# Query products of both layers in plain float32 from an unsplit copy of the normed input; in layer 1 the expert blocks computed ahead as well

## The chip, the cores and the metric
The kernel runs on one core of one Trainium2 chip. The metric is the device time of one execution in microseconds. A core has TensorE (PE; its weight loads are PEld), VectorE (DVE), ScalarE (ACT), GpSimd (POOL) and SyncE (SP), which issues most of the DMAs.

## What is computed
Two layers of a hybrid diffusion backbone on 256 latent and 256 context tokens of width 1024. A layer is a mixer sublayer (four groups of heads, an output projection, a residual and a layer norm) and then an expert layer with product keys, which is the part that the change touches:
```python
def block(hb):                       # 128 tokens, hb: normed and modulated input
    q = (hb @ wq).reshape(PEER_BLOCK, PEER_HEADS, 2, PEER_QDIM // 2)
    s = jnp.einsum('thpk,hpnk->thpn', q, sub_keys).astype(jnp.float32)
    v1, i1 = lax.top_k(s[:, :, 0], K)
    v2, i2 = lax.top_k(s[:, :, 1], K)
    cand = (v1[..., :, None] + v2[..., None, :]).reshape(PEER_BLOCK, PEER_HEADS, K * K)
    cv, ci = lax.top_k(cand, K)
    e = ...                          # expert number from i1, i2 at ci
    g = jax.nn.softmax(cv, -1).reshape(PEER_BLOCK, PEER_HEADS * K)
    act = jax.nn.gelu(jnp.einsum('td,ted->te', hb, u_tab[e]).astype(jnp.float32))
    w = (g * act).astype(hb.dtype)
    return jnp.einsum('te,ted->td', w, v_tab[e])
```
There are 8 heads, 128 keys per half, 16384 experts and 16 picks per head. Layer 0 works on all 512 tokens (four tiles of 128), layer 1 on the 256 latent ones (two tiles).

## The kernel before, in words
All arithmetic is float32. A large product is made of three instructions per 128 rows of the contraction: each operand is split into a rounded half `hi` and a remainder `lo` of type float32r, and `mm3` (L140 to L143) adds hi x hi, hi x lo and lo x hi. `split` (L136 to L138) makes the halves: a cast on ScalarE (L137) and a subtraction on VectorE or GpSimd (L138). Small products (scores, transposes, the modulation products at L260) take unsplit float32 operands.

The expert layer runs in these steps.
- `to_hT` (L781) transposes the normed tokens `x_n` on TensorE, applies scale and shift into `h` on VectorE and ScalarE in turn, and splits `h` into the two halves `hT[0]` and `hT[1]`. In layer 0 it also transposes tile 3 back for the gathered path (`h2n`).
- The routing loop `for q in range(17)` (L1137) alternates `wq(q)` (L1038: load 512 KB of weights into `w_raw`, split with the subtraction on GpSimd, 8 x `mm3` over all NT columns, 512 in layer 0 and 256 in layer 1, copy `qs`) and `top(q - 1)` (L1046: the score product `ss`, a copy to one of two `s_` buffers, and five VectorE instructions per tile for the 16 best). After each four, `pairs(j)` (L1071) combines the halves of two heads on VectorE. One step of the modulation products (`next(fill)`) is made per round in layer 0; `fill_to` (L1150) makes the rest after the loop.
- `u_stage(bl)` (L1006) computes block `bl` of 128 experts for all dense tokens (384 columns in layer 0, where tile 3 takes the gathered path, 256 in layer 1): load `u_raw`, split it, 8 x `mm3` into the bank `au`, gelu into `act`. Of the 128 blocks, 26 in layer 0 and 38 in layer 1 are computed ahead (UA + UB): UA (2, 12) right after the routing loop, UE (7, 6) before the first gates, one after a set of gates where `UM` says so, the others after all gates. GpSimd makes most of their subtractions.
- `slots` (L1172) transposes the picks (`tr`), `hots` (L1182) makes hot rows, and `gates(t, tb)` (L1198) multiplies them on VectorE (L1206, L1209; two buffers each), adds them on TensorE (bank `G`), copies to `stg` and stores to `Gd` in DRAM: 8 per tile.
- The main loop (L1345) computes block `st` ahead by UA + UB, multiplies block `bl` of `act` by its gates (loaded from `Gd` into `gt`), splits the result and the value rows (`v_raw`) and adds into `ov`. The last two blocks are added tile by tile at the end.

`u_raw` is a ring of 2 buffers in layer 0 and 3 in layer 1; `w_raw` of 3. The loads of `u_raw` are issued behind the last `wq` load (`late["D"]`), all on SyncE's queue. A scheduler orders each engine's instructions when the kernel is built, after a time line of its own, with the order of the program as priority; the engines then run their queues in that order.

Of the kernel before, what the change touches and what calls it, by code (L numbers as in the profile page):

```python
# [45 lines left out]
WHB = (4, 5)  # L46
WB = 3
FL = 6
FM = 11
LF = 200  # L50
NF = 2
HB = 3
# [31 lines left out]
def tile_hybrid_diffusion(ctx: ExitStack, tc: tile.TileContext, I: dict, out: bass.AP):  # L84
# [695 lines left out]

    def to_hT(tiles, xsrc, cc, hT, p, back=None, hb=2):  # L781

        for t in tiles:
            s = t // 2
            for q in range(2):
                b = bank("xT")
                for j in range(4):
                    k = 4 * q + j
                    T.transpose(b[:, j * 128:(j + 1) * 128], xsrc(t)[:, k * 128:(k + 1) * 128], ident)
                h = mk(p, [128, 4, 128], tag="h", bufs=hb)  # L790
                for j in range(4):
# [6 lines left out]
                sl = slice(t * 128, t * 128 + 128)  # L798
                split(h, hT[0][:, 4 * q:4 * q + 4, sl], hT[1][:, 4 * q:4 * q + 4, sl])
                if back and t in back:  # L800
# [42 lines left out]
    for l in range(2):  # L843
# [161 lines left out]

        def u_stage(bl, eng=None):  # L1006
            raw = mk(up, [128, 8, 128], tag="u_raw", bufs=URB[l])
            with tc.issue_after(late["D"].ins):
                nc.sync.dma_start(raw, I["uT"][l, bl])
            hi = mk(up, [128, 8, 128], F32R, tag="u_hi", bufs=2 + l)  # L1010
            lo = mk(up, [128, 8, 128], F32R, tag="u_lo", bufs=2 + l)
            split(raw, hi, lo, eng)
            b = bank("au")
            for k in range(8):
                mm3(b[:, :ND], hi[:, k, :], lo[:, k, :], hT[0][:, k, :ND], hT[1][:, k, :ND], k == 0, k == 7)
            p, n = rings[0] if bl % (UA[l] + UB[l]) < UA[l] else rings[1]
            a = mk(p, [128, ND], tag="act", bufs=n)
            S.activation(a, b[:, :ND], AF.Gelu_apprx_tanh)
            acts[bl] = a

        with ExitStack() as rt:
            rp = pool("rp", stack=rt)
            sl4 = mk(rp, [128, NTL, 4, 8, 16], name="sl4")
            dec = mk(rp, [128, 3, 16], F16, name="dec")
            nc.sync.dma_start(dec, I["dec"])
            with ExitStack() as wqs:
                wp = pool("wq", bufs=2, stack=wqs)
                rp2 = pool("rp2", bufs=1, stack=wqs)
                if l:
                    prep.clear()  # L1030
                    prep.update(raw=(wp, 2))
                to_hT(range(NTL), lambda t: x_n[:, t, :], lnc, hT, rp2, {3: h2n} if GT else None, HB)
                keys = mk(rp2, [128, 16, 128], tag="keys", bufs=1)
# [4 lines left out]
                def wq(q):  # L1038
                    hi, lo = load_w(wp, I["wq"][l, q], bufs=WB)
                    b = bank("pq")  # L1040
                    for k in range(8):
                        mm3(b[:, :NT], hi[:, k, :], lo[:, k, :], hT[0][:, k, :NT], hT[1][:, k, :NT], k == 0, k == 7)
                    sq[q] = mk(rp2, [128, NT], tag="qs", bufs=2)
                    S.copy(sq[q], b[:, :NT])
# [107 lines left out]
                for bl in range(UA[l]):  # L1152
                    u_stage(next(ahead), G)
            xp_s.close()
# [66 lines left out]
            for _ in range(UE[l]):  # L1221
                u_stage(next(ahead), V if UEV[l] else G)
            for i, t in enumerate(DT):
                for tb in range(8):
                    gates(t, tb, *cur)
                    if i + 1 < len(DT):
                        if tb == 2:
                            nxt = slots(DT[i + 1])
                        elif tb == 7:
                            nxt = hots(nxt)  # L1230
                    if tb % 8 in UM[l]:
                        for bl in ahead:
                            u_stage(bl, G)
                            break
                cur = nxt
            for bl in ahead:
                u_stage(bl)

# [290 lines left out]
```

## Time and profile before
| | us |
|---|---|
| three runs: lowest, median, highest | 2938.61, 2943.63, 2950.1 |
| the profiled execution | 2948.22 |
| its span, first to last instruction | 2946.4 |

Busy in the profiled execution: TensorE 2656.8 us (90% of the span), VectorE 2099.5 (71%), ScalarE 1164.1 (40%), GpSimd 778.3 (26%). Its mean granted TensorE clock is 0.957 of full speed. In time: layer 0's mixers to 400 us, its routing to 623, gates and blocks ahead to 805, main loop to 1750; layer 1's mixers to 2045, routing to 2187, gates and blocks ahead to 2323, main loop to the end.

A chain of waits names, from the end backwards, what released each step. Matmuls are pipelined: a busy time of TensorE holds the tail of its last instruction, and the pitch of a series is read from the starts.

### The profile page before, as it was taken

The numbers are of one execution on the slowest core, as the hardware profiler recorded it, in microseconds if no ns is written. First come the engines' busy times: TensorE is split into PE (matmuls) and PEld (weight loads), VectorE is DVE, ScalarE is ACT, GpSimd is POOL, SyncE is SP. The second block draws the span as 40 slices with busy tenths as digits, with TensorE's granted clock in tenths as the row PEclk, the third lists the DMA queues.
The fourth block names the chain that finished last, engine by engine and source line by source line (L and its number), as shares of the span: only waits on it lengthen the run. The fifth ranks groups of instructions, "written<-read, shape, count | busy, mean of one in ns | idle before, by whom it ended". The sixth has DMA issues, their size and how long they took to land.

```text
span 2946.4 us, 41926 instructions
## 1 busy us (share of the span) xinstructions
PE 2656.8 (90%) x15646; PEld 2286.7 (78%) x15646; DVE 2099.5 (71%) x4255; ACT 1164.1 (40%) x1810; POOL 778.3 (26%) x505
## 2 busy tenths in 40 slices
PE   6798879688899999999999998788778999999997
PEld 3674557478899988888888987656777999999986
DVE  4956448989687778777767646964999865555556
ACT  2333533235433333333333334334345544444443
POOL 2333013134224444444334103321564100000000
PEclk9899989889899999999999999998888999999999
DMA  7122434336899999988889645325336986666656
GB/s 255 57 90 94 150 122 137 112 117 245 286 334 311 326 321 321 319 307 302 305 308 308 200 129 179 119 82 183 115 116 231 319 272 202 217 209 210 200 181 197
DMA packets 241840, 625.08 MB, mean 212 GB/s; under 512 B 22424, under 2 KB 104794, under 8 KB 236004
## 3 DMA queue, kind: packets, MB, share of 16 engines
q1 hardware_dynamic: 201156, 475.05, 48.6%
q0 software_dynamic: 40480, 147.36, 14.1%
q8 instruction: 122, 2.00, 0.3%
q14 instruction: 82, 0.67, 0.1%
HBM read 573.04 MB, written 49.30 MB: 211 GB/s over the span
## 4 chain that ended last, share of the span: by engine, by line
PE 46%; DVE 20%; DMA 14%; issue 12%; POOL 5%; ACT 3%; SPq 0%; POOLq 0%; DVEq 0%; ACTq 0%
DMA grow<-in_vg_dram,eu 8%; PE ov L142 6%; PE ov L141 6%; PE ov L143 5%; POOL grow L1311 5%; PE au L141 4%; PE au L143 4%; PE au L142 4%; DVE yT L365 2%; PE pj L141 1%; PE pj L142 1%; PE pj L143 1%; DMA wa_raw<-in_w_ada_dram 1%; DVE accg L1324 1%; DVE e L1067 1%
## 5 line engine op out<-in xcount | busy, mean ns | idle before, releaser
L143 PE MATMUL au<-hT,u_lo 128*128 128x384 f32 (+1 forms) x2048 | 642.0, 314 | 12.6 <-POOL u_lo L138 10.0
L141 PE MATMUL au<-hT,u_hi 128*128 128x384 f32 (+1 forms) x2048 | 645.4, 315 | 6.4 <-ACT u_hi L137 3.4
L142 PE MATMUL au<-hT,u_hi 128*128 128x384 f32 (+1 forms) x2048 | 641.5, 313 | 0.0
L142 PE MATMUL ov<-v_lo,wh 128*128 128x512 f32 x1280 | 505.2, 395 | 28.2 <-DVE v_lo L138 27.8
L143 PE MATMUL ov<-v_hi,wl 128*128 128x512 f32 x1280 | 500.1, 391 | 0.0
L141 PE MATMUL ov<-v_hi,wh 128*128 128x512 f32 x1280 | 462.9, 393 | 5.9 <-ACT wh L137 5.6
L137 ACT CAST u_hi<-u_raw 128x1024 fp32r<-128x1024 f32 x256 | 268.7, 1050 | 496.1 <-PE au L142 319.8
L141 PEld LDWEIGHTS au<-hT,u_hi 128*128 128x128 f32 x2048 | 394.1, 192 | 15.3 <-ACT u_hi L137 4.2
L143 PEld LDWEIGHTS au<-hT,u_lo 128*128 128x128 f32 x2048 | 393.2, 192 | 15.6 <-POOL u_lo L138 10.9
L142 PEld LDWEIGHTS au<-hT,u_hi 128*128 128x128 f32 x2048 | 394.1, 192 | 7.7
L138 DVE TENSOR_TENSOR v_lo<-v_raw,v_hi 128x1024 fp32r<-128x1024 f32 x255 | 312.8, 1227 | 79.4 <-ACT v_hi L137 79.1
L138 DVE TENSOR_TENSOR u_lo<-u_raw,u_hi 128x1024 fp32r<-128x1024 f32 x198 | 242.0, 1222 | 148.1 <-ACT u_hi L137 148.1
L137 ACT CAST v_hi<-v_raw 128x1024 fp32r<-128x1024 f32 x256 | 268.3, 1048 | 143.2 <-DMA v_raw<-in_v_dram 109.5
L142 PEld LDWEIGHTS ov<-v_lo,wh 128*128 128x128 f32 x1280 | 241.8, 189 | 84.2 <-DVE v_lo L138 40.9
L137 ACT CAST wh<-act 128x384 fp32r<-128x384 f32 (+1 forms) x256 | 116.9, 459 | 431.1 <-PE ov L142 419.7
L141 PEld LDWEIGHTS ov<-v_hi,wh 128*128 128x128 f32 x1280 | 242.0, 190 | 51.4 <-ACT wh L137 5.9
L143 PEld LDWEIGHTS ov<-v_hi,wl 128*128 128x128 f32 x1280 | 241.5, 189 | 49.7
L138 POOL TENSOR_TENSOR w_lo<-w_raw,w_hi 128x1024 fp32r<-128x1024 f32 (+1 forms) x72 | 176.9, 2466 | 251.5 <-ACT w_hi L137 219.6
L138 POOL TENSOR_TENSOR u_lo<-u_raw,u_hi 128x1024 fp32r<-128x1024 f32 x58 | 171.4, 2961 | 257.3 <-ACT u_hi L137 250.8
L1311 POOL DMA_INDIRECT grow<-in_vg_dram,eu x128 | 179.0, 1398 | 221.5 <-DVE accg L1324 167.2
L1311 POOL DMA_INDIRECT grow<-in_ug_dram,eu x128 | 160.6, 1255 | 262.8 <-DVE grow L1315 232.2
L1324 DVE SCALAR_TENSOR_TENSOR accg<-grow,ag,accg 128x1024 f32<-128x1024 f32 x127 | 162.8, 1282 | 75.8 <-DMA grow<-in_vg_dram,eu 75.1
(832 smaller groups left out, 4324.9 us busy)
## 6 DMA issues: line engine op xcount, KB each, us to landing
u_raw<-in_uT_dram SPq DMA_DIRECT2D x256, 512.0 KB
v_raw<-in_v_dram SPq DMA_DIRECT2D x256, 512.0 KB
Gd<-stg SPq DMA_DIRECT2D x40, 1024.0 KB
gt<-Gd SPq DMA_DIRECT2D x80, 512.0 KB
wa_raw<-in_w_ada_dram SPq DMA_DIRECT2D x76, 512.0 KB
w_raw<-in_w_in_t_dram SPq DMA_DIRECT2D x44, 512.0 KB
w_raw<-in_wq_dram SPq DMA_DIRECT2D x32, 512.0 KB
w_raw<-in_w_ada_dram SPq DMA_DIRECT2D x20, 512.0 KB
```

Of the source, the lines that this page charges most:

```text
L137: S.copy(hi, src)
L138: late["V" if eng in (None, V) else "G"] = (eng or V).tensor_tensor(lo, src, hi.bitcast(F32), ALU.subtract)
L141: T.matmul(o, lh, rh, start=first, stop=False)
L142: T.matmul(o, lh, rl, start=False, stop=False)
L143: return T.matmul(o, ll, rh, start=False, stop=last)
L365: V.scalar_tensor_tensor(uc, upad[:, m, :, j:j + 256], wj, uc, op0=ALU.mult, op1=ALU.add)
L1067: V.tensor_tensor(x[:, :, :, 0:w], x[:, :, :, 0:w], x[:, :, :, w:2 * w], ALU.add)
L1311: nc.gpsimd.indirect_dma_start(out=r, out_offset=None, in_=I[tab], in_offset=bass.IndirectOffsetOnAxis(ap=eu[:, i:i + 1], axis=0))
L1324: V.scalar_tensor_tensor(accg, r, ag[:, i:i + 1], accg, op0=ALU.mult, op1=ALU.add)
```

## The change
With `PW` the routing of both layers keeps an unsplit copy of the normed input, `h32` (in layer 0 tiles 0 to 2; tile 3 in `h32g`), and `wq` multiplies the raw weights by it in plain float32, with `w_raw` as a ring of 4 and 5 buffers (`PRB`) and no halves of the weights. The halves `hT`, which the blocks need, are made from the copy after product 1, in four pieces, with the subtraction on VectorE; those of layer 0's tile 3, which only the query products read, are gone. With `PU` the 38 blocks ahead of layer 1 are plain too: no `u_hi`, no `u_lo`, `u_raw` read by TensorE. The blocks of layer 0 and those of both main loops stay split.
```diff
--- before.py
+++ after.py
@@ -45,6 +45,9 @@
 NE = 2
 WHB = (4, 5)
 WB = 3
+PW = (1, 1)
+PU = (0, 1)
+PRB = (4, 5)
 FL = 6
 FM = 11
 LF = 200
@@ -778,7 +781,7 @@
         run(ssd(), attention(), hyena(), conf_norm(), more)
         mp_s.close()
 
-    def to_hT(tiles, xsrc, cc, hT, p, back=None, hb=2):
+    def to_hT(tiles, xsrc, cc, hT, p, back=None, hb=2, h32=None):
 
         for t in tiles:
             s = t // 2
@@ -787,7 +790,7 @@
                 for j in range(4):
                     k = 4 * q + j
                     T.transpose(b[:, j * 128:(j + 1) * 128], xsrc(t)[:, k * 128:(k + 1) * 128], ident)
-                h = mk(p, [128, 4, 128], tag="h", bufs=hb)
+                h = h32(t)[:, 4 * q:4 * q + 4, :] if h32 else mk(p, [128, 4, 128], tag="h", bufs=hb)
                 for j in range(4):
                     k = 4 * q + j
                     sc, sh = cc[:, 0, k, s:s + 1], cc[:, 1, k, s:s + 1]
@@ -796,7 +799,8 @@
                     else:
                         V.tensor_scalar(h[:, j, :], b[:, j * 128:(j + 1) * 128], sc, sh, op0=ALU.mult, op1=ALU.add)
                 sl = slice(t * 128, t * 128 + 128)
-                split(h, hT[0][:, 4 * q:4 * q + 4, sl], hT[1][:, 4 * q:4 * q + 4, sl])
+                if not h32:
+                    split(h, hT[0][:, 4 * q:4 * q + 4, sl], hT[1][:, 4 * q:4 * q + 4, sl])
                 if back and t in back:
                     b = bank("hb")
                     for j in range(4):
@@ -1003,16 +1007,24 @@
         rings = [(up, UA[l])]
         gsl = {}
 
-        def u_stage(bl, eng=None):
+        def u_stage(bl, eng=None, plain=False):
             raw = mk(up, [128, 8, 128], tag="u_raw", bufs=URB[l])
             with tc.issue_after(late["D"].ins):
                 nc.sync.dma_start(raw, I["uT"][l, bl])
+            if plain:
+                b = bank("au")
+                for k in range(8):
+                    T.matmul(b[:, :ND], raw[:, k, :], h32[0][:, k, :ND], start=k == 0, stop=k == 7)
+                return act_of(bl, b)
             hi = mk(up, [128, 8, 128], F32R, tag="u_hi", bufs=2 + l)
             lo = mk(up, [128, 8, 128], F32R, tag="u_lo", bufs=2 + l)
             split(raw, hi, lo, eng)
             b = bank("au")
             for k in range(8):
                 mm3(b[:, :ND], hi[:, k, :], lo[:, k, :], hT[0][:, k, :ND], hT[1][:, k, :ND], k == 0, k == 7)
+            act_of(bl, b)
+
+        def act_of(bl, b):
             p, n = rings[0] if bl % (UA[l] + UB[l]) < UA[l] else rings[1]
             a = mk(p, [128, ND], tag="act", bufs=n)
             S.activation(a, b[:, :ND], AF.Gelu_apprx_tanh)
@@ -1022,6 +1034,9 @@
             rp = pool("rp", stack=rt)
             sl4 = mk(rp, [128, NTL, 4, 8, 16], name="sl4")
             dec = mk(rp, [128, 3, 16], F16, name="dec")
+            h32 = []
+            if PW[l]:
+                h32.append(mk(rp, [128, 8, ND], name="h32"))
             nc.sync.dma_start(dec, I["dec"])
             with ExitStack() as wqs:
                 wp = pool("wq", bufs=2, stack=wqs)
@@ -1029,17 +1044,35 @@
                 if l:
                     prep.clear()
                     prep.update(raw=(wp, 2))
-                to_hT(range(NTL), lambda t: x_n[:, t, :], lnc, hT, rp2, {3: h2n} if GT else None, HB)
+                if PW[l] and GT:
+                    h32.append(mk(rp2, [128, 8, 128], name="h32g"))
+
+                def cols32(t):
+                    return h32[1] if t in GT else h32[0][:, :, t * 128:(t + 1) * 128]
+                to_hT(range(NTL), lambda t: x_n[:, t, :], lnc, hT, rp2, {3: h2n} if GT else None, HB, cols32 if PW[l] else None)
                 keys = mk(rp2, [128, 16, 128], tag="keys", bufs=1)
                 nc.sync.dma_start(keys, I["keys"][l])
                 n8 = 2 * NTL
                 vs, ixs, sq = {}, {}, {}
 
                 def wq(q):
-                    hi, lo = load_w(wp, I["wq"][l, q], bufs=WB)
                     b = bank("pq")
-                    for k in range(8):
-                        mm3(b[:, :NT], hi[:, k, :], lo[:, k, :], hT[0][:, k, :NT], hT[1][:, k, :NT], k == 0, k == 7)
+                    if PW[l]:
+                        raw = mk(wp, [128, 8, 128], tag="w_raw", bufs=PRB[l])
+                        late["D"] = nc.sync.dma_start(raw, I["wq"][l, q])
+                        o = 0
+                        for h in h32:
+                            n = h.shape[-1]
+                            for k in range(8):
+                                T.matmul(b[:, o:o + n], raw[:, k, :], h[:, k, :], start=k == 0, stop=k == 7)
+                            o += n
+                        if q == 1:
+                            for i in range(0, 8, 2):
+                                split(h32[0][:, i:i + 2, :], hT[0][:, i:i + 2, :ND], hT[1][:, i:i + 2, :ND])
+                    else:
+                        hi, lo = load_w(wp, I["wq"][l, q], bufs=WB)
+                        for k in range(8):
+                            mm3(b[:, :NT], hi[:, k, :], lo[:, k, :], hT[0][:, k, :NT], hT[1][:, k, :NT], k == 0, k == 7)
                     sq[q] = mk(rp2, [128, NT], tag="qs", bufs=2)
                     S.copy(sq[q], b[:, :NT])
 
@@ -1150,7 +1183,7 @@
                 fill_to(1, (FL, 11)[l])
                 ahead = iter(range(min(UA[l] + UB[l], 128)))
                 for bl in range(UA[l]):
-                    u_stage(next(ahead), G)
+                    u_stage(next(ahead), G, PU[l])
             xp_s.close()
             if l == 0:
                 fwp_s.close()
@@ -1219,7 +1252,7 @@
 
             cur = hots(slots(DT[0]))
             for _ in range(UE[l]):
-                u_stage(next(ahead), V if UEV[l] else G)
+                u_stage(next(ahead), V if UEV[l] else G, PU[l])
             for i, t in enumerate(DT):
                 for tb in range(8):
                     gates(t, tb, *cur)
@@ -1230,11 +1263,11 @@
                             nxt = hots(nxt)
                     if tb % 8 in UM[l]:
                         for bl in ahead:
-                            u_stage(bl, G)
+                            u_stage(bl, G, PU[l])
                             break
                 cur = nxt
             for bl in ahead:
-                u_stage(bl)
+                u_stage(bl, None, PU[l])
 
 
         UBl = UA[l] + UB[l]
```

## Rows read from the trace of the kernel before
**Rows 1.** By stretch: busy us of PE, PEld, DVE, ACT, POOL; clock, DMA share, GB/s
```profile
437.00:520.00 83.00, 81.12 (x424) 59.34 (x424) 71.09 (x383) 27.23 (x38) 30.17 (x12) 1.00 0.43 138
520.00:607.00 87.00, 59.05 (x358) 39.33 (x357) 84.48 (x521) 19.46 (x25) 5.77 (x3) 0.77 0.38 127
2055.00:2186.00 131.00, 100.41 (x734) 97.64 (x734) 120.10 (x536) 55.15 (x88) 67.19 (x27) 0.88 0.36 116
2186.00:2214.00 28.00, 20.24 (x148) 20.14 (x149) 23.67 (x20) 10.80 (x17) 20.17 (x7) 0.80 0.45 139
2214.00:2306.00 92.00, 80.17 (x879) 77.69 (x879) 85.83 (x53) 51.67 (x94) 35.91 (x13) 0.93 0.70 241
2323.00:2900.00 577.00, 575.87 (x3535) 518.15 (x3535) 353.03 (x572) 278.90 (x416) 6.79 (x9) 1.00 0.69 222
```
**Rows 2.** Instructions of L1116, 2055 to 2310 us: duration in ns, min/median/max, first and last start
```profile
L1116 DVE TENSOR_TENSOR e<-e,dec x4: 674/1750/2914, 2092.1 to 2179.3; 128x1024 f16<-128x1024 f16 x4
```
**Rows 3.** Timeline, 2150 to 2160 us: start, length, engine, line, instruction, [idle before]
```profile
2150.80 7.58 POOL L138 TENSOR_TENSOR u_lo<-u_raw,u_hi 128x1024 fp32r<-128x1024 f32 x3 [3.38 <-ACT u_hi L137]
...
2153.23 2.91 DVE L1116 TENSOR_TENSOR e<-e,dec 128x1024 f16<-128x1024 f16 x1
```
**Rows 4.** Groups of GpSimd, 2045 to 2323 us: busy us, mean ns | idle before, releasers
```profile
L138 POOL TENSOR_TENSOR u_lo<-u_raw,u_hi 128x1024 fp32r<-128x1024 f32 x34 | 91.6, 2702 | 89.9 <-ACT u_hi L137 85.9 <-PE au L142 2.2 <-PE G L1216 1.8
```
**Rows 5.** Chain of waits, 395 to 660 us (layer 0): start, length in us, what
```profile
410.62 2.76 DVE hT L138
...
423.51 0.72 PE pq L141 x2
...
453.05 0.89 PE ss L1050 x8
...
460.31 0.89 PE ss L1050 x8
...
568.03 0.89 PE ss L1050 x8
...
569.55 3.64 DMA wa_raw<-in_w_ada_dram
...
623.17 0.45 PE tr L1175
```
**Rows 6.** Timeline of TensorE: plain float32 products of 512, 256 and 128 columns
```profile
223.06 1.98 PE L528 MATMUL uf<-yT,dft 128*128 128x512 f32 x4
...
276.25 1.89 PE L555 MATMUL yi<-dft,hT 128*128 128x256 f32 x8
...
434.92 1.05 PE L1050 MATMUL ss<-keys,qs 128*128 128x128 f32 x8
```
**Rows 7.** Timeline of TensorE, from 2141 us: split products of 256 columns
```profile
2140.81 0.28 PE L143 MATMUL au<-hT,u_lo 128*128 128x256 f32 x1
2140.93 0.28 PE L141 MATMUL au<-hT,u_hi 128*128 128x256 f32 x1
```
**Rows 8.** Chain of waits, 2035 to 2420 us (layer 1): start, length in us, what
```profile
2055.26 0.58 PE pq L142
...
2066.17 0.44 PE ss L1050 x4
2069.43 0.44 PE ss L1050 x4
...
2186.76 0.48 PE tr L1175
...
2214.50 0.59 PE G L1215 x4
...
2307.20 7.69 DMA Gd<-stg
...
2315.37 6.88 DMA v_raw<-in_v_dram
...
2323.38 1.19 PE ov L141 x4
```

## The prediction
> **What bounds the kernel now.** I read the busy time by stretch first, then the chain of waits through the two routing stages, then the timeline. Each layer ends in a long expert loop that TensorE fills: in layer 1 it is busy 575.87 of 577 us at a granted clock of 1.00 (2.4 GHz) [rows 1]. So whatever brings the start of that loop forward comes off the end, and whatever delays it is added. The change touches only what stands ahead of the two loops: query products with their top-16 search ("routing"), gates, and blocks computed ahead. There it is not TensorE that is full. From 2055 to 2306 us TensorE is busy 100 of 131, 20 of 28 and 80 of 92 us, at mean granted clocks of 0.88, 0.80 and 0.93, while VectorE is busy 120, 24 and 86 [rows 1]; the chain there runs almost wholly through VectorE. In layer 0 TensorE is full from 437 to 520 (81 of 83), then VectorE is (84 of 87) [rows 1].
>
> VectorE is partly held up. The same comparison (L1116, 1024 columns) takes 674 ns at its fastest and 2914 at its slowest, among four in layer 1 [rows 2], and the slow one begins at 2153.23, while GpSimd runs three `u_lo` subtractions from 2150.80 to 2158.38 [rows 3]. I took each VectorE instruction's duration less the tenth percentile of its own form. The excess is 45 us between 2055 and 2186, 41 us from there to 2310 and 31 us in layer 0 between 437 and 623. Nearly all of it lies on instructions with two tensors as input and on copies, casts and scalar forms; the `MAX8` searches lose next to nothing. GpSimd has 34 `u_lo` subtractions in layer 1's stretch [rows 4] and 16 of `w_lo`, one per query product: 86 / 50 = 1.7 us lost per subtraction, between 0 and 2.2 (2914 less 674) by the row. The Trainium skill (SBUF — State Buffer, Who interferes with whom) says that the two engines share one pair of ports, held for a whole instruction. By that rule, which the rows bear out, the excess goes with the subtractions.
>
> **The change, part by part.**
> (a) *A plain product against a split one.* Split: three instructions per 128 rows of the contraction, 0.12 us apart at 256 columns [rows 7], so 24 x 0.12 = 2.88 us per block. Plain: the trace records each such product as two instructions (48 records of L555 for the 24 in the code). Eight take 1.89 us at 256 columns, the last 0.38 of it its own tail, so 1.51 / 7 = 0.216 us apart; four at 512 take 1.98 with a tail of 0.59 and a slow first step, so 0.43 apart; eight at 128 take 1.05 with a tail of 0.28, so 0.11 apart [rows 6]. A block of 256 columns then costs 16 x 0.216 = 3.46, +0.58 us. Layer 0's query product is 384 + 128 columns: 16 x (0.323 + 0.11) = 6.93 us, where 384 is taken between 0.216 and 0.43. Before, the step from one query product to the next is 460.31 - 453.05 = 7.26 us, of which 1.0 is the score product and 0.65 the modulation product [rows 5]: 5.61, so +1.32 us. TensorE thus gets 16 x 1.32 = 21 us more work in layer 0 and (16 + 38) x 0.58 = 31 us more in layer 1. The edit is a loss on the engine that bounds the kernel unless these stretches have room.
> A rule of the Trainium skill would turn that sum round: TensorE: Matmul & The Clock Gate (Measured speedup vs the span model) says that a weight load overlaps a running matmul only if it goes to other rows of the array. With that page's 128 / 1.2 = 107 ns per load as an estimate, 16 plain passes would cost 5.2 us against 5.4 for 24 split ones. The rows show no such load in series: 0.216 us apart, with new weights for each record. By the rule layer 1's 54 products would cost 15 us less instead of 31 more, which gives 2899 - 46 = 2853; chance 0.01.
>
> (b) *The way into the query products.* Removed: the halves of `hT` ahead of them. In layer 0 one such subtraction alone took 2.76 us at 410.62 [rows 5], and the `w_hi` casts stood between the `h` casts on ScalarE. Transposes begin at 403.4; 32 `h` instructions shared by VectorE (0.42 us) and ScalarE then end near 412, so the first product starts near 411.5, not at 423.5 [rows 5]: -12 us. In layer 1 the products run from 2055.26 [rows 8]; they would from about 2050: -5. The split of the unsplit copy moves behind product 1: four casts and four VectorE subtractions, some 3 to 4 us on an engine that then waits for the second score product; nothing, and at most 4 if the order puts them into a full stretch.
>
> (c) *Layer 0's routing.* TensorE alone: 16 x 6.93 + 15 x 1.0 + 8.5 (modulation) + 10.6 (its rows and columns) = 145 us from 411.5, so product 15 ends near 557, against 568.03 [rows 5]: -11. VectorE needs 4.8 us for each top-16 and 16.5 for each set of pairs without the excess. Fed at 8.6 us per product, it ends near 589 against 622. What is late next is the chain of modulation products that waits for one weight load after the other (3.64 us at 569.55 [rows 5]) and holds TensorE until 607; it starts 11 us earlier and ends near 596. The 5 us in which TensorE then waits for the slots' transpose (623.17 [rows 5]) go too. Layer 0's blocks keep their split, so the rest of its gates is as before. Sum: -15; bounds -3 (start only 6 us earlier, and the order of the queues keeps the wait) and -22.
>
> (d) *Layer 1's routing.* Score products follow 3.26 us apart (2066.17, 2069.43 [rows 8]) and would 3.9 apart. VectorE is continuously busy from 2074 to the transpose at 2186.76 [rows 8], 112 us, of which 45 is excess. Replayed without it, and with the first search 5 us earlier, it ends near 2138. TensorE ends product 15 near 2121, being held by the two buffers of scores. So the bound passes from VectorE to TensorE.
>
> (e) *Layer 1's blocks ahead and gates.* 18 blocks stand before the first gate: 18 x 3.46 = 62 us, so the first gate product is at 2184, against 2214.50 [rows 8]. Then 16 times gate (1.9) and block (3.46), 86 us where the trace has 91. The last gate ends near 2270, against 2306. From its copy-out to the loop's first product runs the store of the gates, 7.69 us, and the load of `v_raw`, 6.88, to 2323.38 [rows 8]: unchanged, so the loop's products start 36 us earlier. But TensorE had two of the loop's own blocks done by then, 2 x 2.9 us, and would not have. Sum: -30. Bounds: with no idle TensorE at all it needs 62 + 131 + 30 + 1 = 225 us from 2050, -42; with the load limit below, -7.
> The `u_raw` ring: a buffer was free after cast and subtraction, now after the product. The SyncE queue issues the next load only then, and gate stores stand behind it. A load has 2 x 3.46 = 6.9 us to land. The rows have 3.64 and, under load, 6.88 [rows 5, 8]. I take it as hidden; if loads take 10.7 us, a block takes (10.7 + 3.46) / 3 = 4.7, which costs 18 x 1.27 = 23 us.
>
> **Sum.** -15 - 30 = -45 us from the profiled execution, 2948.2 us (span 2946.4), so 2903. That execution lies 4.6 above the median of the runs, 2943.6; against the median I predict 2899.
>
> **The rivals.**
> 1. *Room fully used*: the order of the queues fills every gap of TensorE: -42 and -22, so 2880. For it: 15 or more us of the stretch are at the lower clock (1.2 GHz), after idle time, and that goes with the gaps. Against: the score buffers still tie TensorE to VectorE. Chance 0.13.
> 2. *Loads of `u_raw` become the wait*, as priced: 2899 + 23 = 2922. For it: a ring of three that is held longer. Against: the DMA engines are busy 0.36 to 0.70 of the time there [rows 1]. Chance 0.10.
> 3. *Slower: TensorE is the bound and gets no room.* Its 21 + 31 us are paid in full, and only the earlier starts (12 and 5) come back: 2943.6 + 35 = 2979. It decides if VectorE's excess is not GpSimd's doing, or if the rewritten order leaves the slots' transposes and the hot rows behind the 18 blocks and TensorE then waits as long as before. For it: what makes an instruction long is inferred from what runs beside it, and no stretch of routing runs without GpSimd. Against: slow and fast copies of one instruction, with and without GpSimd beside them. Chance 0.06.
> 4. *The gain is there and is lost again* at the two entries to the loops, where the store of gates and two loads follow each other, or in one of the layers for the order of the queues: within 0.5%, 2940. Chance 0.08.
>
> **How the numbers follow.** Forecast 0.62 (2899, own range 2884 to 2915), rivals 0.13, 0.10, 0.06, 0.08, the weight-load rule 0.01. Range 2872 to 2930: it takes in rivals 1 and 2 and leaves out 3 and 4. About 0.5%, 14.7 us, is what a measurement of this kernel can tell from no change. Faster by more than that: forecast, 1, 2 and the rule, 0.86. Same: 0.08. Slower: 0.06.
>
> **What would show it.** (a) `au` of layer 1's blocks ahead as 16 records 0.216 us apart, a block of 3.46 us. (b) First query product near 411 in layer 0. (c, d) No GpSimd subtraction between 402 and 557 or between 2035 and the loop, and L1116 at one duration there; the time from layer 1's first query product to the slots' transpose down from 131 us to 115 or less, with TensorE at clock 1.00. (e) First gate product some 130 us after the first query product, not 160. The forecast is wrong if VectorE's long instructions stay long with GpSimd idle, if TensorE waits for `u_raw`, or if its queue holds the gates behind blocks that it could have run earlier.

## The result

The changed kernel takes 2902.57 us, median of 4 runs (2897.7 to 2908.49), against 2945.79 for the kernel before on the same chip: ratio 0.9857, 95% interval 0.9826 to 0.9887. The forecast was 2899. The profiled execution of the changed kernel took 2899.02 us, its span is 2897.2; all stage times below are from profiled executions.

Five points in TensorE's queue cut both traces into stages (starts of instructions; the last column is what the stage that ends there gained or lost):

| us | before | after | change of the stage |
|---|---|---|---|
| layer 0: first `pq` | 423.16 | 410.72 | -12.4 |
| layer 0: first `ov` | 805.56 | 789.75 | -3.4 |
| layer 1: first `pq` | 2052.52 | 2034.29 | -2.4 |
| layer 1: first `ov` | 2323.4 | 2272.8 | -32.4 |
| last product | 2931.19 | 2882.12 | +1.5 |

By stretch, the changed kernel, with the columns of [rows 1]:
```profile
411.00:520.00 109.00, 107.59 (x554) 71.09 (x553) 80.08 (x495) 25.48 (x40) 0.00 (x0) 1.00 0.37 117
520.00:605.00 85.00, 64.79 (x422) 42.36 (x421) 79.42 (x443) 21.12 (x26) 6.15 (x2) 0.79 0.47 156
2034.00:2142.00 108.00, 106.11 (x514) 93.42 (x514) 87.47 (x553) 34.93 (x70) 0.00 (x0) 0.98 0.41 128
2142.00:2164.00 22.00, 22.00 (x111) 19.33 (x110) 11.11 (x11) 3.18 (x9) 0.00 (x0) 1.00 0.49 145
2164.00:2246.00 82.00, 82.00 (x753) 74.42 (x751) 53.07 (x47) 38.66 (x81) 0.00 (x0) 1.00 0.81 291
2273.00:2850.00 577.00, 576.18 (x3530) 518.69 (x3531) 349.88 (x565) 275.60 (x412) 6.79 (x9) 1.00 0.71 221
```
In layer 1 GpSimd (the fifth busy time) is at nought from 2034 to 2246, TensorE is full in all three stretches (106 of 108, 22 of 22, 82 of 82) at a clock of 0.98 to 1.00, and VectorE, which was full before, has room: 53 of 82 in the gates. The bound passed from VectorE to TensorE.

The comparison of [rows 2], same view (ns, min/median/max), now L1149:
```profile
L1149 DVE TENSOR_TENSOR e<-e,dec x4: 681/684/694, 2065.2 to 2122.3; 128x1024 f16<-128x1024 f16 x4
```
All four are short, where they ran from 674 to 2914. Each VectorE instruction's duration less the tenth percentile of its form in the changed kernel gives an excess of 83.0 us before and 5.8 after, between layer 1's first query product and its last gates.

The chain of waits of the changed kernel in layer 1, against [rows 8] (start, length in us, what):
```profile
2030.95 3.50 PE xT L792 x16
2034.45 7.00 PE pq L1067 x32
...
2042.19 3.46 PE pq L1067 x16
2045.65 0.44 PE ss L1083 x4
...
2099.78 42.80 PE au L1017 x192
2142.58 0.44 PE tr L1208 x4
2143.02 20.72 PE au L1017 x96
2165.58 3.51 PE au L1017 x16
...
2240.73 3.51 PE au L1017 x16
2246.07 10.43 PE au L1017 x48
2256.52 3.67 DMA u_raw<-in_uT_dram
2260.21 1.05 ACT u_hi L140
2261.28 1.24 DVE u_lo L141
2262.54 3.76 DMA u_raw<-in_uT_dram
...
2268.62 1.83 DVE act L1286 x9
...
2272.80 2.07 PE ov L144 x4
```
The reader is to see three things. The chain no longer runs through VectorE from the last searches to the gates, but through `au`. A plain block is 3.46 us (16 records), as worked out. And the entry to the loop has become another: the chain passes two loads of `u_raw` and the splits of two of the loop's own blocks, where it passed the store of the gates and the load of `v_raw` before [rows 8]. From the last gates product to the first `ov` it takes 26.9 us, against 17.8.

In layer 0, TensorE's timeline in the changed kernel from product 15 on (start, length, instruction, [idle before and what ended it]); it answers to the last rows of [rows 5]:
```profile
557.40 1.06 PE L1083 MATMUL ss<-keys,qs 128*128 128x128 f32 x8
558.39 1.50 PE L263 MATMUL pm<-wa_raw,s 128*32 128x256 f32 x24
567.46 2.08 PE L1083 MATMUL ss<-keys,qs 128*128 128x128 f32 x8 [7.57 <-ACT qs L1077]
569.33 1.91 PE L281 MATMUL pt<-sel,rw 128*128 128x128 f32 x8
571.17 2.50 PE L263 MATMUL pm<-wa_raw,s 128*32 128x256 f32 x24
576.09 0.64 PE L263 MATMUL pm<-wa_raw,s 128*32 128x256 f32 x8 [2.42 <-DMA wa_raw<-in_w_ada_dram]
...
603.31 2.08 PE L281 MATMUL pt<-sel,rw 128*128 128x128 f32 x8 [1.07 <-ACT rw L267]
605.04 0.67 PE L144 MATMUL au<-hT,u_hi 128*128 128x384 f32 x1
```
Product 15 ends at 557.5 as forecast, but TensorE then stands 7.57 us before the last score product, and the modulation chain behind it ends at 605.0, not at 596. What it stands for is seen on ScalarE (same columns):
```profile
554.67 0.59 ACT L1085 COPY s__704_3987<-ss 128x512 f32<-128x512 f32 x1
565.02 1.90 ACT L1158 CAST e<-tf 128x2048 f16<-128x2048 f32 x1 [9.77 <-DVE tf L1157]
566.83 0.58 ACT L1077 COPY qs<-pq 128x512 f32<-128x512 f32 x1
567.78 0.60 ACT L267 COPY rw<-pm 128x512 f32<-128x512 f32 x1
```
The copy `qs` of product 15, and the copy `rw` that the modulation chain's next step reads, stand in ScalarE's queue behind a cast of the third set of pairs, and that cast waits 9.77 us for VectorE.

### The profile page after: what moved, and what is told of

Read it like the earlier page. It is cut to its first block, busy times and chain, and to the rows that moved or that the text cites. A ratio compares the mean times of both kernels' runs of the same rounds, so it can differ in the third digit from the quotient of the medians.

```text
span 2897.2 us, 41097 instructions
## 1 busy us (share of the span) xinstructions
PE 2688.0 (93%) x15342; PEld 2283.5 (79%) x15342; DVE 1996.6 (69%) x4247; ACT 1098.8 (38%) x1736; POOL 595.0 (21%) x439
## 4 chain that ended last, share of the span: by engine, by line
PE 39%; DMA 13%; issue 11%; DVE 9%; POOL 6%; ACT 1%; SPq 0%; POOLq 0%; DVEq 0%; ACTq 0%
DMA grow<-in_vg_dram,eu 9%; PE ov L144 5%; PE ov L145 5%; POOL grow L1344 5%; PE ov L146 5%; PE au L1017 4%; PE au L144 4%; PE au L146 4%; PE au L145 4%; DMA grow<-in_lnr_dram 2%; DVE accg L1357 1%; DVE yT L368 1%; PE G L1248 1%; PE G L1249 1%; DMA grow<-in_ug_dram,eu 1%
## 5 line engine op out<-in xcount | busy, mean ns | idle before, releaser
L146 PE MATMUL au<-hT,u_lo 128*128 128x384 f32 (+1 forms) x1744 | 552.6, 317 | 5.6 <-DVE u_lo L141 5.2
L144 PE MATMUL au<-hT,u_hi 128*128 128x384 f32 (+1 forms) x1744 | 553.4, 317 | 3.0 <-DVE slT L1212 3.0
L145 PE MATMUL au<-hT,u_hi 128*128 128x384 f32 (+1 forms) x1744 | 551.6, 316 | 0.0
L140 ACT CAST u_hi<-u_raw 128x1024 fp32r<-128x1024 f32 x218 | 228.9, 1050 | 447.0 <-PE au L145 303.7
L144 PEld LDWEIGHTS au<-hT,u_hi 128*128 128x128 f32 x1744 | 332.1, 190 | 11.0 <-DVE slT L1212 3.4
L146 PEld LDWEIGHTS au<-hT,u_lo 128*128 128x128 f32 x1744 | 331.6, 190 | 9.6 <-DVE u_lo L141 8.3
L145 PEld LDWEIGHTS au<-hT,u_hi 128*128 128x128 f32 x1744 | 331.9, 190 | 7.7
L1348 DVE SCALAR_TENSOR_TENSOR grow<-grow,h2n 128x1024 f32<-128x1024 f32 x128 | 156.0, 1222 | 59.8 <-DMA grow<-in_ug_dram,eu 59.7
L141 DVE TENSOR_TENSOR wl<-act,wh 128x384 fp32r<-128x384 f32 (+1 forms) x256 | 125.3, 491 | 101.8 <-ACT wh L140 100.5
```

What stands on the lines that cost most here:

```text
L140: S.copy(hi, src)
L141: late["V" if eng in (None, V) else "G"] = (eng or V).tensor_tensor(lo, src, hi.bitcast(F32), ALU.subtract)
L144: T.matmul(o, lh, rh, start=first, stop=False)
L145: T.matmul(o, lh, rl, start=False, stop=False)
L146: return T.matmul(o, ll, rh, start=False, stop=last)
L1348: V.scalar_tensor_tensor(r, r, 1.0, h2n, op0=ALU.mult, op1=ALU.mult, accum_out=ag[:, i:i + 1])
```

## The experiments

The theory of the prediction: the gain is VectorE's excess, which GpSimd's subtractions cause; plain products are the means by which they go, and cost TensorE time. The rival that it left open: the plain products are worth something themselves. All runs below are against the kernel before on the same chip; not all were on one chip, so two runs are compared by their ratios or by their stages.

| run | median us | ratio to before | 95% interval | layer 1, first `pq` to `ov`, us |
|---|---|---|---|---|
| before | 2945.79 | | | 270.9 |
| after | 2902.57 | 0.9857 | 0.9826 to 0.9887 | 238.5 |
| l0_only | 2934.09 | 0.9956 | 0.9938 to 0.9973 | 271.5 |
| wq_only | 2912.15 | 0.9894 | 0.9852 to 0.9936 | 251.2 |
| split_on_vector | 2910.3 | 0.9868 | 0.983 to 0.9906 | 236.1 |
| plain_gpsimd | 2921.38 | 0.9907 | 0.9877 to 0.9936 | 254.3 |
| all_plain | 2906.17 | 0.9871 | 0.9847 to 0.9895 | 238.6 |
| gates_on_pool_queue | 2909.0 | 0.9878 | 0.9852 to 0.9905 | 244.0 |
| last4_split | 2894.57 | 0.9816 | 0.9771 to 0.9861 | 232.9 |
| l0_plain_l1_vector | 2899.98 | 0.9853 | 0.9829 to 0.9877 | 234.6 |
| wq_plain_u_vector | 2889.45 | 0.9814 | 0.9794 to 0.9833 | 225.5 |
| wq_plain_u_vector_both | 2877.23 | 0.9759 | 0.9718 to 0.98 | 227.7 |
| both_again (the same kernel) | 2877.24 | 0.9746 | 0.9705 to 0.9787 | 227.0 |
| all_on_vector | 2885.28 | 0.9781 | 0.9749 to 0.9813 | 236.3 |

**Parts of the change alone.** `l0_only`, only layer 0's query products plain:
```diff
-PW = (1, 1)
-PU = (0, 1)
+PW = (1, 0)
+PU = (0, 0)
```


> Layer 0's query products alone are plain; layer 1 is as before. Theory (the gain is VectorE freed from GpSimd, in both layers, and an earlier start of the query products): layer 0 gives its own 15 to 16 us, so about 2930 us where before has 2946, and layer 0's main loop starts near 790 instead of 805 in the profile. Rival (all of the gain lies in layer 1, where GpSimd had 50 subtractions, and layer 0 only pays 21 us more TensorE work): 2946 or more.

Measured 0.9956, some 13 us of the 43. Layer 1's stage is as before, 271.5 us.

`wq_only`, the query products of both layers plain, no blocks:
```diff
-PU = (0, 1)
+PU = (0, 0)
```


> Query products of both layers are plain, layer 1's blocks ahead stay split with their subtraction on GpSimd. Theory: 16 of the 50 subtractions of layer 1 are gone, all of them in the routing, so its VectorE chain is some 25 us shorter and the gates keep their stalls: 16 + 20 to 25 us in all, near 2908 (2900 to 2918). Rival (the blocks ahead carry layer 1's gain): near 2930, as with layer 0 alone.

Measured 0.9894. From layer 1's first query product to `ov` 251.2 us: of the 32.4 us that the change gains there, 19.7 come with the query products and 12.7 with the blocks. Where GpSimd still works, VectorE is still held up: in this run's gates GpSimd subtracts for 47.4 us, and VectorE's excess there is 33.0 us. The group of GpSimd, 2176 to 2268 us (busy us, mean ns | idle before):
```profile
L141 POOL TENSOR_TENSOR u_lo<-u_raw,u_hi 128x1024 fp32r<-128x1024 f32 x16 | 47.4, 2969 | 36.4 <-ACT u_hi L140 34.6 <-PE G L1249 1.8
```

**GpSimd's subtractions taken away without plain products.** `split_on_vector` is the kernel before, with layer 1's subtractions on VectorE:
```diff
-                    hi, lo = load_w(wp, I["wq"][l, q], bufs=WB)
+                    hi, lo = load_w(wp, I["wq"][l, q], eng=V if l else G, bufs=WB)
-                    u_stage(next(ahead), G)
+                    u_stage(next(ahead), V if l else G)
-                            u_stage(bl, G)
+                            u_stage(bl, V if l else G)
```
and `UEV = (0, 1)`.

> The kernel before, all products split, but in layer 1 the subtractions of the query weights and of the blocks ahead are made on VectorE instead of GpSimd. Theory (a GpSimd subtraction holds up VectorE by 1.7 us, more than the 1.22 us that the subtraction takes on VectorE itself): VectorE loses 86 us of stalls and gets 50 x 1.22 = 61 us of work, so its chain is about 25 us shorter and the time 10 to 25 us lower: near 2928. Rival (the long VectorE instructions have another cause): the 61 us come on top of a full VectorE, near 3000.

Measured 0.9868, as good as the change within the intervals, without any plain product; the theory had asked for 10 to 25 us and got 37. Layer 1's stage is 236.1 us, 2.4 below the change's. The comparison L1116 in this run:
```profile
L1116 DVE TENSOR_TENSOR e<-e,dec x4: 672/680/685, 2089.4 to 2162.1; 128x1024 f16<-128x1024 f16 x4
```
A subtraction takes VectorE 1.22 us; beside one on GpSimd it had lost more than that (83.0 us of excess beside 47 subtractions in that stretch).

The run takes away two things at once: VectorE's excess, and GpSimd's longer subtraction (2702 ns in the mean [rows 4]), for which a product waits. In the kernel before the second is small in layer 1: TensorE stands 3.2 us at GpSimd's `u_lo` in the routing and not at all in the gates, where its 18.8 us of idle time end at VectorE's products.

**GpSimd's subtractions put back.** `plain_gpsimd` is the changed kernel, where GpSimd makes a subtraction of the same size per query product and per block ahead of layer 1:
```diff
             if plain:
+                G.tensor_tensor(mk(up, [128, 8, 128], F32R, tag="u_lo", bufs=2 + l), raw, raw, ALU.subtract)
                 b = bank("au")
...
                         late["D"] = nc.sync.dma_start(raw, I["wq"][l, q])
+                        if l:
+                            G.tensor_tensor(mk(wp, [128, 8, 128], F32R, tag="w_lo", bufs=2), raw, raw, ALU.subtract)
```


> The kernel after, with one subtraction of raw weights on GpSimd per query product and per block ahead of layer 1, whose result nobody reads: all products as after, GpSimd as busy as before. Theory (VectorE's stalls are what the change removes in layer 1): its gain is gone and TensorE's 31 us more are not hidden any longer, so layer 1 is as before or up to 15 us slower, with layer 0's 16 us kept: 2930 to 2945. Rival (the gain is the cast and the subtraction that stood between load and product, or the casts on ScalarE): as after, near 2903.

Measured 0.9907, between the theory and the rival: some 15 us slower than the change by the ratios, 15.8 by layer 1's stage. VectorE's excess is back: 28.9 us from the first query product to the transposition of the picks, 2.3 from there to the first gates, 24.2 in the gates, with 26, 6 and 16 subtractions beside it: 55.4 / 48 = 1.15 us each, or 1.03 above the 5.8 us that the stretch keeps without any. But the excess in the gates does not show in the time. This run by stretch, routing and gates:
```profile
2035.00:2153.00 118.00, 108.86 (x515) 94.59 (x515) 111.17 (x547) 32.65 (x66) 55.22 (x27) 0.97 0.38 118
```
```profile
2180.00:2262.00 82.00, 82.00 (x751) 74.31 (x749) 76.18 (x47) 38.36 (x80) 37.85 (x16) 1.00 0.80 290
```
To the first gates product it takes 144.6 us against 129.3. TensorE's idle time there ends at the copies `qs` (9.1 us) and at VectorE's picks (3.7), none of it at a load, so it is not that GpSimd holds the buffers longer. The gates take 82.3 us, to a tenth as without GpSimd: VectorE is busy 76 there instead of 53, but TensorE is full with plain blocks and sets the pace. So it is shown, in both directions, that GpSimd's subtraction lengthens VectorE's instructions, and that in layer 1 this costs time only where VectorE is the bound.

The Trainium skill (SBUF — State Buffer, Who interferes with whom) says that a VectorE instruction with two inputs in SBUF contends with a GpSimd instruction that reads SBUF. `plain_gpsimd` bears it out, by 1.15 us of excess for each subtraction; how the two share the ports within an instruction, no run here shows.

**The loop's entry.** Was it the order of SyncE's queue, where the gates' loads stand behind five loads of `u_raw`? `gates_on_pool_queue` issues layer 1's gates' loads from GpSimd's queue:
```diff
-                        nc.sync.dma_start(gts[i], Gd[i][:, :, bl * TB:(bl + GB) * TB].rearrange("a p c -> p a c"))
+                        (nc.gpsimd if l else nc.sync).dma_start(gts[i], Gd[i][:, :, bl * TB:(bl + GB) * TB].rearrange("a p c -> p a c"))
```


> The kernel after, with layer 1's loads of the gates (gt from Gd) issued from GpSimd's queue, which is empty there, instead of SyncE's. Theory (layer 1's loop starts 26.9 us after the last gate product instead of 17.8 because the gate loads stand in SyncE's queue behind five loads of u_raw, each of which waits for a product to free its buffer): that stretch falls back to 17 to 20 us and the time by 7 to 9, to about 2894. Rival (the loop's first blocks wait for the u_raw loads themselves and their two halves): 27 us and 2902 as after.

That fell: the stretch from the last gates product to `ov` is 32.5 us, not shorter than 26.9, and the gates' load is issued at 2271.28 from a queue with nothing ahead of it. GpSimd's queue stands until the last plain product ends, at 2270.76, and the load follows 0.5 us later: it waits for that product and not for SyncE's queue. That it wants memory which the product still reads is likely, but not shown. The run's chain of waits:
```profile
2253.43 10.43 PE au L1017 x48
2263.88 3.58 DMA u_raw<-in_uT_dram
2267.47 1.05 ACT u_hi L140
2268.55 1.24 DVE u_lo L141
...
2271.65 10.93 DMA u_raw<-in_uT_dram
...
2284.98 0.21 DVE act L1286
```
The chain is again that of the loads of `u_raw`, each of which waits until a plain product gives a buffer back; the product with the gates (L1286) stands on VectorE behind the split of those blocks. So the last plain blocks were split again, in `last4_split`:
```diff
             for bl in ahead:
-                u_stage(bl, None, PU[l])
+                u_stage(bl)
```


> The changed kernel, with the four layer 1 expert blocks that stand behind the last gates made from split halves again (the copies on ScalarE, the subtractions on VectorE, 24 float32r products each); everything ahead of them stays plain. In the changed kernel the layer 1 loop's first ov product began 26.9 us after the last gates product, against 17.8 before, and the five last u_raw transfers wait for plain products that free their buffers. Theory (the loop's first gate and value transfers are held by the last plain products, which read u_raw and the float32 copy h32 until they end; split blocks free u_raw after a copy and a subtraction, and h32 is not read after the gates): from the last gates product to ov about 17.5 us, from the first layer 1 query product to ov about 229 us, time about 2893 us. Rival (the entry is late because the gates end earlier, and the transfers' own round trip sets it): about 27 us, 238 us and 2902 us.

Measured 0.9816 and 21.4 us from the last gates product to `ov`: 5.5 of the 9.1 us are the last four plain blocks' doing, and layer 1's stage falls by 5.6 to 232.9. The theory holds for its larger part; it asked for 17.5. The chain at the entry in this run:
```profile
2246.73 6.72 DMA u_raw<-in_uT_dram
...
2254.55 1.24 DVE u_lo L141
...
2257.86 4.06 SPq L1294
...
2262.44 5.71 DMA v_raw<-in_v_dram
```
One load of `u_raw` is left in it, from 2246.7 on, when the last plain block beside the gates ends, and SyncE's queue stands 4.06 us at a load of `v_raw`. For what that load waits was not tried.

**More and fewer plain products.** `all_plain`, layer 0's blocks plain too:
```diff
-PU = (0, 1)
+PU = (1, 1)
```


> The kernel after, with layer 0's 26 blocks ahead plain as well. A block of 384 columns costs 16 x 0.323 = 5.2 us instead of 4.3, so TensorE gets 22 us more between 605 and 790, where it is busy nearly all the time (26 blocks and 24 gate products are some 160 of 185 us). Theory (a plain product pays where TensorE has room and costs where it has none): slower than after by 5 to 18 us, 2907 to 2920. Rival (GpSimd's silence pays there too, as in layer 1): 2890 or less.

Measured 0.9871: nothing gained over the change (0.9857). In layer 0 the stretch from the last gates product to `ov` is 28.5 us, against 22.4 to 23.8 in all eight runs with layer 0 as in the change: plain blocks lengthen that entry as well.

`wq_plain_u_vector` keeps the query products plain and makes layer 1's blocks ahead from halves, subtracted on VectorE:
```diff
-PU = (0, 1)
-UEV = (0, 0)
+PU = (0, 0)
+UEV = (0, 1)
...
-                    u_stage(next(ahead), G, PU[l])
+                    u_stage(next(ahead), V if l else G, PU[l])
```
(and the same at the blocks between the gates).

> Query products of both layers plain as after, layer 1's blocks ahead split as before but with their subtraction on VectorE. Theory (what counts in layer 1 is GpSimd's silence; the plain blocks cost 22 us of TensorE work that is no longer hidden, since TensorE is now the bound there): from layer 1's first query product to its loop some 220 us, against 238.5 after and 251.2 with the subtractions on GpSimd; about 2886. Rival (VectorE is nearly full, and 38 x 1.22 = 46 us more of it come on top): 255 us or more, 2920.

Measured 0.9814, and 225.5 us for layer 1's stage, 13.0 less than the change's 238.5. To the first gates product it takes 131.9 us against 129.3 (+2.6), the gates 76.3 against 82.3 (-6.0), the entry 17.4 against 26.9 (-9.5): where TensorE is the bound, a plain block costs time, and then again at the entry.

`l0_plain_l1_vector` has layer 0's query products plain and everything in layer 1 split, on VectorE:
```diff
-PW = (1, 1)
-PU = (0, 1)
-UEV = (0, 0)
+PW = (1, 0)
+PU = (0, 0)
+UEV = (0, 1)
```
(and `V if l else G` for layer 1's query weights and blocks).

> Layer 0's query products plain, layer 1 all split with the subtractions on VectorE. Theory (the two gains are apart and add): layer 1 takes 236 us from its first query product to its loop, as with the subtractions moved alone, and layer 0's 13 us come on top of that run's 2910: about 2897, as fast as the change or a little faster. Rival (the gains overlap): 2905 to 2910.

Measured 0.9853; layer 1's stage 234.6 us. Beside `wq_plain_u_vector` that prices layer 1's plain query products alone: 234.6 - 225.5 = 9.1 us gained, nearly all before the transposition of the picks (120.9 against 111.6).

**Layer 0 as well.** `wq_plain_u_vector_both` takes GpSimd's subtractions off layer 0's blocks too (the edit is against `wq_plain_u_vector`):
```diff
-                    u_stage(next(ahead), V if l else G, PU[l])
+                    u_stage(next(ahead), V, PU[l])
-UEV = (0, 1)
+UEV = (1, 1)
```
(and the same at the blocks between the gates).

> Query products plain in both layers as in the change, expert blocks ahead split in both layers, with the subtraction on VectorE in layer 0 too (in the change and in the run with VectorE's subtraction in layer 1 alone, layer 0's is GpSimd's). In layer 0 of the changed kernel the stretch from the first transposition of the routing's result to the last gates product took 152.9 us. Theory (a GpSimd subtraction costs VectorE more than the same subtraction on VectorE does, wherever VectorE is bound): layer 0's first ov product a few us sooner than 789.7 us, time 2882 to 2889 us. Rival (in layer 0 TensorE, and the gap to the loop, set the end, so that nothing is gained or the few extra VectorE instructions are in the way): 2889 to 2894 us, ov at 789 to 793 us.

Measured 0.9759, below the theory's range, first `ov` of layer 0 at 781.0 us. It was taken again, as `both_again`:

> The run with plain query products and VectorE's subtractions for the blocks ahead in both layers, taken again beside the run without any plain product. Theory (layer 0's stretch from the routing's transposition to the last gates product is shorter by some 9 to 17 us without GpSimd's subtractions, in every execution): that stretch 140 to 144 us again, time 2874 to 2882 us. Rival (the 141.96 us of the first execution was the low end of a spread that reached from 150.9 to 159.8 us with GpSimd's subtractions): 148 us or more, time 2884 us or more.

Measured 0.9746; from the transposition to the last gates product 141.8 us, after 142.0. With GpSimd's subtractions for layer 0's blocks, and the rest of layer 0 the same, it was 151 to 160 in eight runs, the change among them. The gates' two products per set in layer 0, in the changed kernel (614 to 768 us) and in this one (620 to 762; xcount | busy us, mean ns | idle before):
```profile
L141 POOL TENSOR_TENSOR u_lo<-u_raw,u_hi 128x1024 fp32r<-128x1024 f32 x21 | 60.1, 2860 | 84.2 <-ACT u_hi L140 81.6 <-PE G L1248 2.6
...
L1239 DVE TENSOR_TENSOR Ah<-o,o 128x2048 f16<-128x2048 f16 x24 | 41.7, 1745 | 15.2 <-PE G L1248 15.2
L1239 DVE TENSOR_TENSOR Al<-o,o 128x2048 f16<-128x2048 f16 x24 | 35.5, 1487 | 0.0
```
```profile
L1239 DVE TENSOR_TENSOR Ah<-o,o 128x2048 f16<-128x2048 f16 x24 | 29.0, 1217 | 0.0
L1239 DVE TENSOR_TENSOR Al<-o,o 128x2048 f16<-128x2048 f16 x24 | 28.9, 1216 | 0.0
L141 DVE TENSOR_TENSOR u_lo<-u_raw,u_hi 128x1024 fp32r<-128x1024 f32 x22 | 26.8, 1219 | 24.0 <-ACT u_hi L140 21.5 <-PE G L1249 2.5
```
The subtraction itself takes 1219 ns on VectorE and 2860 on GpSimd, and the 48 products lose 19.3 us to it; all of VectorE's instructions in the stretch, each against the tenth percentile of its form in `both_again`, lose 36.1 us beside the 21 subtractions, 1.7 each.

Here VectorE's excess is not the whole of it. In four of the eight runs TensorE waits 6.8 to 9.4 us for GpSimd's `u_lo`, in the other four 2.6 or less. The longest, `plain_gpsimd` (618 to 778 us; us in total, times, longest):
```profile
PE au L146 <- POOL u_lo L141: 9.4, 3, 6.8
```
Those four take 157 to 160 us, with GpSimd's subtraction at 3369 to 3613 ns and VectorE's excess at 27.5 to 31.8 us. The others take 151 to 154 us, with 2747 to 3008 ns and 32.5 to 38.7 us. So VectorE loses less where GpSimd and TensorE lose more. A subtraction on VectorE removes both, and no run tells them apart in layer 0.

`all_on_vector` asks what the plain products bring at all: the kernel before with every one of these subtractions of both layers on VectorE (the diff of `split_on_vector`, with V in place of `V if l else G`, and `UEV = (1, 1)`).

> The kernel before, with no plain product at all: every query product and every block ahead of both layers stays split, and its subtraction is made by VectorE instead of GpSimd. What is asked is how much of the gain the plain products themselves bring, beyond taking GpSimd off. Theory (nearly all of the gain is GpSimd's subtractions gone from beside a bound VectorE; the plain products add only the way into layer 0's routing, 12 us, and some us of layer 1): layer 0's first query product at 423 to 425 us as before, layer 0's first ov product at 790 to 797 us (805.6 before), layer 1 from query product to ov about 236 us as in the run with VectorE's subtractions in layer 1 alone, time 2890 to 2902 us. Rival (in layer 0 VectorE is bound in the routing and 16 more subtractions of 1.22 us stand on its path): first ov product at 803 us or later, time 2908 us or more.

Measured 2885.28 us, 0.9781: below the theory's range, and with an interval apart from the change's. So the rival that the plain products bring the gain falls: a kernel without one is faster than the change by 17 us in the medians and 22 by the ratios. What plain query products are worth on top is seen beside `both_again` from the same chip: layer 1's stage 227.0 against 236.3 us, layer 0's first `ov` 782.1 against 781.1. In layer 0 they start 7 us sooner (413.15 against 419.94) and lose it again. The intervals of the two ratios overlap, so the 8 us between the medians rest on the stage times.

## Why the prediction was right, and where it was not

- **(a) The price of a plain product**: right. Blocks of 3.46 us, score products 3.46 + 0.44 = 3.90 us apart, product 15 of layer 0 ends 147 us after the first product begins (145 in the sum). The rule of the Trainium skill on weight loads (TensorE: Matmul & The Clock Gate, where it stands in the section The mechanism) is not borne out: 48 records in 10.43 us are 0.217 us each, with new weights for each.
- **(b) The way in**: right in layer 0 (410.72 for 411.5). In layer 1 the products begin 3.34 us after the transposes, against 6.84 before (2045.68 to 2052.52): -3.5, -5 in the sum. The 2055.26 of [rows 8], from which the sum counts, is a later step of the first query product, which starts at 2052.52. The stage from `ov` to the first query product as a whole gave -2.4.
- **(c) Layer 0's routing**: the sum of -15 met the -15.8 of the profiled execution by luck, not by its steps. Two of them failed. A set of pairs was put at 16.5 us of VectorE's time and takes 20.7 (four sets 82.9 us; the searches cost 16 x 4.7, near the 4.8 that were put down), so VectorE's routing ended at 601.5 us, not 589. And the modulation chain was to start 11 us earlier and end near 596. Its step behind the last score product began at 569.33, only 2 us before the 571.28 of the kernel before, since ScalarE's copies stand behind a cast that waits for VectorE; from there it takes 36 us, as before, and ended at 605.0. From the first query product to the transposition of the picks layer 0 became longer, from 200.0 to 203.9 us, and 204 to 207 in the other seven runs with the same layer 0. Part of that is only moved: two blocks (605.0 to 614.8) now stand ahead of the transposition on TensorE, which came behind it before. The gates after it made good for it in this execution: with the same code the first `ov` came between 789.8 and 800.9 us in eight executions, 795.7 in the mean. The kernel before's layer 0 gave 805.6 and, in `split_on_vector`, 800.1. Layer 0's share by that is nearer -7 to -10 than -15; `l0_only` gives -13 in time, by its interval -8 to -18.
- **(d) Layer 1's routing**: right. VectorE's routing ended at 2128.2 us, 94 after the first query product, where 88 was worked out and 134 had been; TensorE has no gap worth the name. One term was off: product 15 was to end near 2121, 71 us after the first began, held by the score buffers; it was not held, and the blocks ahead began at 2099.8, 65 us after it. That VectorE's long instructions were GpSimd's doing is shown by `split_on_vector` and `plain_gpsimd`.
- **(e) Blocks and gates**: right in sum, with one step wrong. First gates product 129.3 us after the first query product (134 in the sum, which had product 15 held), the gates 82.3 us for 86; but the entry was put down as unchanged and cost 9.1 us more. The two own blocks that were to be missing at the end show as 1.5 us, not 5.8. The rival of `u_raw` was looked for in the wrong place: TensorE never waits for it between 2034 and 2246 us, where the 10.7 us per load were feared, and the chain runs through its loads at the entry, where the ring is still held by plain products while the loop's own blocks want it.
- **Rival 3** (slower) fell with VectorE's excess, 83.0 to 5.8 us; **rival 4** (lost again at the entry) is there, with 9 us of 43; **rival 1** (2880) was not reached by the change, since TensorE's extra work fills the room that it makes.

What the prediction did not ask: whether the subtraction could go elsewhere for less. On VectorE it costs 1.22 us, less than the 1.7 lost per subtraction that the prediction itself counted. Best of all measured is plain query products with all blocks ahead split on VectorE: 2877 us, 0.9746 and 0.9759.

## What to carry to other kernels

Before an engine's work is removed, ask what it costs its neighbour: here one subtraction on GpSimd lengthened VectorE's work by 1.15 to 1.7 us, about as much as VectorE takes to do it (1.22) or more. Take it off only where the neighbour is the bound, and try the cheapest way first, which was the other engine and not another kind of product. When a buffer is held longer, look at the next user of its ring behind the stage, not only at the stage itself.

## What was not expected of the hardware

- The same stretch of layer 0 (transposition to last gates product) took 150.9 to 159.8 us in eight executions of the same instructions with GpSimd's subtractions beside VectorE's; in the two without, 142.0 and 141.8. The longer ones are those in which TensorE waits for GpSimd, not those in which VectorE loses most.
- 24.2 us of VectorE's excess in the gates of `plain_gpsimd` cost nothing: 82.3 us either way.
- GpSimd's own subtraction grows too: in `plain_gpsimd` 1890 ns at its shortest, 2038 in the mean beside the searches and 2366 beside the gates; 2860 in layer 0's gates of the changed kernel. The Trainium skill (GPSIMD Engine Reference, 4.1 Engine selection) puts a two-input operation at about twice VectorE's time; these rows give 1.7 to 2.3 times its 1.22 us.
